# A hybrid diffusion network on one core: scans and projections dealt out block by block, and a new head ahead of them

## The chip, the cores and the metric

The kernel runs on one core of a Trainium2 chip. A core has a matrix engine (TensorE, PE in the profile), three engines for elementwise work (VectorE is DVE, ScalarE is ACT, GpSimd is POOL) and a queue that issues transfers (SyncE, SP); ScalarE and GpSimd can issue transfers too. The engines run side by side, each works through its own instructions in a fixed order, and they wait for each other by semaphores. TensorE writes to PSUM, eight banks of 512 numbers for each of 128 partitions; SBUF is the working memory. The metric is the time of one execution in microseconds (us).

## The reference, cut to what matters

Two layers work on 1024 latent tokens and 256 context tokens of width 1024. The first has a Mamba-2 mixer (SSD), the second attention, and a mixture of experts follows each. Only the first layer's mixer is touched here:

```python
h = rmsnorm(x, norm1_w) * (1 + scale) + shift     # shift, scale: silu(c) @ ada_w + ada_b
z, xbc, dtr = split(h @ in_w)                     # widths 2048, 4096, 64
xs, B, C = split(silu(dwconv(xbc, width=5)))      # 32 heads of 64; 8 groups of 128 states
dt = softplus(dtr + dt_bias); A = -exp(A_log)     # for a forward and a backward scan
y = scan_forward(xs, dt, A, B, C) + scan_backward(...) + D_skip * xs
out = rmsnorm(y * silu(z)) @ out_w
```

Each scan is chunked, with 128 tokens to a chunk. Inside a chunk y is a product of a decay matrix (times C·B) with x; between chunks a state is stepped on and read through C.

## The kernel before

All matrices are float32. A product of full precision is made of three: each operand is split into a rounded part and a remainder (`split`: ScalarE copies and rounds, VectorE or GpSimd subtracts), and `mm3` multiplies high by high, high by low and low by high.

**The head.** `ssd` loads the tokens in three blocks of 256, 512 and 512 (`BLK`), with transfers of 256 rows. `ada` makes shift and scale: eight pieces of the weights, 1 MB each, come through three buffers (`adw`), and each is multiplied as it lands. A loop over the ten token tiles makes the norm, scales on VectorE, transposes on TensorE and copies the result out of PSUM into `hf` (line 203 on ScalarE, line 205 on VectorE). Once shift and scale are known, a second loop modulates `hf` in SBUF (line 218, lines 216 for two of eight columns) and splits it into `hh` and `hl`, which every projection reads. Then follow `dt`: its projection (line 256), an eviction into `dT` by ScalarE, ten transposes (`dps`, line 261) to which VectorE adds `dtb` (`dt_bias`, line 262), and a long chain on VectorE that ends in the decays. The small loads for it, `dcol` (D), `dtb` and `nega` (A_log), stand on ScalarE's queue behind the modulation (lines 238, 245, 247).

**The projections.** `conv_tile` makes one tile of 128 channels: it loads and splits 512 KB of weights, and projects the three token blocks by `proj`, 24 matmuls each, into one of three PSUM banks (`in_ps`). ScalarE evicts each block twice (lines 358, 359). VectorE then runs the convolution: four passes over 1284 columns (line 363) and, around a tanh, two over 642 (line 368). `next(mods)` at its start advances the modulation for the rest of the layer by one piece.

**The scans.** There are eight groups. Each makes a B tile and a C tile, transposes B (`Btm`), multiplies C by B for each chunk (line 527, evicted into `cb`), and then for each of two pairs of heads makes an x tile and calls `core`. `core` transposes x (line 377), runs the backward states (lines 410, 396), and then goes through five pairs of chunks in seven iterations: `decays` for pair i (a transfer `Eb`, two selects on GpSimd, eight exponentials on ScalarE, an addition on GpSimd, a product with `cb` on VectorE, line 431: this gives M), `forward` for pair i (line 443 and the state's step, line 396), `entering` for pair i-1 (line 456: states read through C), and `output` for pair i-2: four y matmuls on M (line 474), an identity matmul that adds the entering part (line 477), and VectorE's `yd`, which is stored.

**The gates.** `gate` projects a tile of z, multiplies y with its silu, stores it and sums squares. Two of the sixteen (`early`) are made in the scans' pools after the last core, the rest behind them while `out_w` is loaded.

**What sets the order.** The program text is a trace of instructions. A scheduler then fixes each engine's queue ahead of time: it plays the trace against a cost model and gives an engine that is free the earliest traced instruction which the model holds to be ready and for which buffers are free. So matmuls traced later fill gaps that the model sees, but on the chip a queue waits for whatever stands at its front. `tc.issue_after(i)` places what is traced in its block behind instruction i on the same engine, in order only.

These lines of `core` are the ones that the change deals with:

```python
for i in range(len(pairs) + 2):
    if i < len(pairs):
        M[i] = decays(pairs[i])
        ent[i] = forward(pairs[i])
    ...
    if i >= 2:
        output(pairs[i - 2], M.pop(i - 2), yos.pop(i - 2), behind)
```

## Time and profile before

| | us |
|---|---|
| median of 3 runs (3855.78 to 3867.84) | 3864.43 |
| the profiled execution | 3858.05 |
| its span, first to last instruction | 3856.3 |

Busy in the span: TensorE 92%, VectorE 68%, ScalarE 53%, GpSimd 45%. The mean granted clock of TensorE was 0.973 of full speed.

In a row, L218 is line 218 of the kernel. PE is TensorE's matmuls, PEld its weight loads; a q behind an engine's name (SPq, ACTq) is its sequencer, which issues transfers. A matmul's end is modelled, so the rate of a stream is read from the starts. "A <- B" says that A's engine sat idle until B was done.

### The profile page before, as it was taken

The page shows a single profiled execution, that of the slowest core. Times are in us where ns is not written, and L with a number is a line of the kernel's source. Part 1 is how long each engine was busy: PE and PEld are TensorE (multiplying, and loading weights), DVE is VectorE, ACT ScalarE, POOL GpSimd, SP SyncE. Part 2 cuts the span into 40 slices and gives each one's busy share as a digit, 9 for nine tenths or more (in the row PEclk, how much of TensorE's full clock was granted, in tenths as well). Part 3 has the DMA queues.
Part 4 walks back from the last instruction along what each step waited for, and adds up shares of the span by engine and source line. Part 5 has one row for each costly group of instructions (what it writes and reads, how often), then busy time and mean ns, then how long its engine had stood idle before and what let it go on. Part 6 is the DMA issues. An engine that isn't in the chain of part 4 may idle for free.

```text
span 3856.3 us, 56522 instructions
## 1 busy us (share of the span) xinstructions
PE 3547.7 (92%) x21153; PEld 2674.9 (69%) x21153; DVE 2612.5 (68%) x3696; ACT 2026.0 (53%) x3325; POOL 1742.6 (45%) x1330
## 2 busy tenths in 40 slices
PE   5999999999899998999999999899999975999997
PEld 3767777777787775666666767677777654777765
DVE  4776777777634377666666665555666577999988
ACT  4545444544333223555555545477777534777665
POOL 1255444554443224566666652221111005777786
PEclk7999999999999998999999999999999987999999
DMA  4333322222544336888888873100000346999994
GB/s 174 105 109 125 118 92 78 83 85 84 154 139 152 110 128 234 307 317 317 320 321 302 289 236 94 36 15 1 1 1 12 132 168 235 378 381 376 352 339 165
DMA packets 296354, 681.07 MB, mean 177 GB/s; under 512 B 24192, under 2 KB 150000, under 8 KB 289936
## 3 DMA queue, kind: packets, MB, share of 16 engines
q1 hardware_dynamic: 269520, 615.50, 44.4%
q0 software_dynamic: 12720, 39.33, 4.2%
q10 hardware_dynamic: 13840, 22.63, 1.8%
q8 instruction: 167, 2.74, 0.3%
q14 instruction: 107, 0.88, 0.1%
HBM read 611.95 MB, written 62.82 MB: 175 GB/s over the span
## 4 chain that ended last, share of the span: by engine, by line
PE 38%; DVE 11%; issue 6%; POOL 4%; DMA 4%; ACT 2%; SPq 0%; ACTq 0%; POOLq 0%; DVEq 0%
DVE m_w L741 6%; PE pv L1189 5%; PE S L1155 4%; PE acc L54 4%; PE a_tr L1176 4%; PE acc L55 4%; PE acc L56 4%; PE cacc L710 4%; POOL m_w L739 3%; DMA m_raw<-in_moe_w_dram 3%; PE o_ps L55 1%; PE o_ps L56 1%; PE o_ps L54 1%; ACT m_w L736 1%; PE qkv L56 1%
## 5 line engine op out<-in xcount | busy, mean ns | idle before, releaser
L741 DVE TENSOR_TENSOR m_w<-m_raw,m_w 128x1792 fp32r<-128x1792 f32 (+1 forms) x384 | 889.7, 2340 | 242.3 <-ACT m_w L736 240.2
L736 ACT ACTIVATE m_w<-m_raw 128x2048 fp32r<-128x2048 f32 x384 | 732.7, 1916 | 477.8 <-DMA m_raw<-in_moe_w_dram 273.5
L739 POOL TENSOR_TENSOR m_w<-m_raw,m_w 128x256 fp32r<-128x256 f32 (+1 forms) x384 | 810.4, 2134 | 354.4 <-ACT m_w L736 353.1
L54 PE MATMUL in_ps<-hh,w 128*128 128x512 f32 (+1 forms) x1152 | 423.1, 367 | 10.9 <-DVE th L505 9.9
L55 PE MATMUL acc<-m_w,xl 128*128 128x512 f32 x1024 | 407.5, 398 | 22.9 <-DVE m_w L741 12.3
L56 PE MATMUL in_ps<-hh,w 128*128 128x512 f32 (+1 forms) x1152 | 420.2, 365 | 0.0
L55 PE MATMUL in_ps<-hl,w 128*128 128x512 f32 (+1 forms) x1152 | 418.3, 363 | 0.0
L54 PE MATMUL acc<-m_w,xl 128*128 128x512 f32 x1024 | 405.7, 402 | 3.0 <-ACT xl L48 2.0
L56 PE MATMUL acc<-m_w,xl 128*128 128x512 f32 x1024 | 402.4, 393 | 0.0
L427 ACT ACTIVATE Eb<-Eb,ebias 128x128 f32<-128x128 f32 x640 | 199.3, 391 | 166.4 <-POOL Eb L422 158.6
L1159 DVE TENSOR_REDUCE mx<-S 128x1 f32<-128x1024 f32 x128 | 155.7, 1217 | 182.1 <-PE S L1155 180.0
L54 PEld LDWEIGHTS in_ps<-hh,w 128*128 128x128 f32 x1152 | 220.0, 191 | 48.7 <-DVE th L505 10.9
L328 POOL TENSOR_TENSOR w<-w_raw,w 128x512 fp32r<-128x512 f32 x96 | 152.6, 1610 | 221.0 <-ACT w L325 210.7
L55 PEld LDWEIGHTS acc<-m_w,xl 128*128 128x128 f32 x1024 | 193.8, 189 | 82.9 <-DVE m_w L741 25.3
L1206 POOL TENSOR_TENSOR q<-s 64x128 f32<-64x128 f32 x128 | 58.5, 457 | 415.0 <-DVE mx L1164 340.2
L56 PEld LDWEIGHTS in_ps<-hh,w 128*128 128x128 f32 x1152 | 219.9, 191 | 31.0 <-issue 5.0
L55 PEld LDWEIGHTS in_ps<-hl,w 128*128 128x128 f32 x1152 | 219.8, 191 | 29.5 <-issue 4.3
L54 PEld LDWEIGHTS acc<-m_w,xl 128*128 128x128 f32 x1024 | 193.0, 189 | 67.3 <-issue 15.7
L56 PEld LDWEIGHTS acc<-m_w,xl 128*128 128x128 f32 x1024 | 193.9, 189 | 38.3 <-DVE xl L49 0.2
L55 PE MATMUL acc<-m_w,gT 128*128 128x512 f32 x512 | 203.8, 398 | 6.7 <-DVE m_w L741 4.1
L54 PE MATMUL acc<-m_w,gT 128*128 128x512 f32 x512 | 201.9, 400 | 1.3 <-ACT gT L48 1.3
L56 PE MATMUL acc<-m_w,gT 128*128 128x512 f32 x512 | 202.1, 395 | 0.1
(385 smaller groups left out, 7626.4 us busy)
## 6 DMA issues: line engine op xcount, KB each, us to landing
m_raw<-in_moe_w_dram SPq DMA_DIRECT2D x384, 1024.0 KB
adw<-in_ada_w_dram SPq DMA_DIRECT2D x48, 1024.0 KB
Eb<-fd SPq DMA_DIRECT2D x80, 512.0 KB
w_raw<-in_ssd_in_w_dram SPq DMA_DIRECT2D x48, 512.0 KB
ydd<-yd SPq DMA_DIRECT2D x80, 128.0 KB
yt_raw<-yzd SPq DMA_DIRECT2D x40, 256.0 KB
xs<-x SPq DMA_DIRECT2D x16, 512.0 KB
h<-h SPq DMA_DIRECT2D x16, 512.0 KB
```

The source lines that it names most:

```text
L54: mm(out, lhs[0], rhs[0], start=start, stop=False)
L55: mm(out, lhs[0], rhs[1], start=False, stop=False)
L56: mm(out, lhs[1], rhs[0], start=False, stop=stop)
L427: nc.scalar.activation(Eb[:, d, hh, cc], Eb[:, d, hh, cc], AF.Exp, bias=bias[:, c0 + cc, k:k + 1])
L710: nc.tensor.matmul(acc[32 * q:32 * q + 32], xc[:, k], raw[:, k % 2, 256 * q:256 * q + 256], start=(k == 0), stop=(k == KT - 1))
L736: nc.scalar.activation(w[0], raw, AF.Copy)
L739: nc.gpsimd.tensor_tensor(w[1][:, :, n:], raw[:, :, n:], w[0][:, :, n:].bitcast(F32), op=OP.subtract)
L741: nc.vector.tensor_tensor(w[1][:, :, :n], raw[:, :, :n], w[0][:, :, :n].bitcast(F32), op=OP.subtract)
L1155: nc.tensor.matmul(o, qTs[self.qt][:, 2 * self.hp + hh], kT[k][:, self.kv, 512 * b:512 * b + n], start=(k == 0), stop=(k == 1))
L1159: nc.vector.tensor_reduce(self.mx[:, 0:1], S[hh], axis=AX.X, op=OP.max)
L1176: nc.tensor.transpose(ps[:, q], self.pr[hh][:, (c0 + q) * P:(c0 + q + 1) * P], net.ident)
L1189: nc.tensor.matmul(self.pv[o:o + 64, 0], v32[:, t, self.kv], self.PT[:, t], start=(t < 2), stop=(t >= NT - 2))
```

## The change

1. The pool `cs` and the loads of `dt_bias`, `A_log` and D move ahead of the head. They land in parts of `wst`, which is not needed until the end of the `dt` chain. D is loaded as whole rows and set in place by two VectorE copies.
2. In the head all eight pieces of `ada` are traced first, then the tokens. The transposes of one column tile of a block share a PSUM bank (three banks instead of two), and the modulation reads that bank: ScalarE writes `hi`, VectorE the full value, and VectorE or GpSimd, in turns, the remainder.
3. `conv_tile` and `gate` become generators that yield after each token block. `core` takes such a sequence (`fill`), asks for one block at the start of each iteration but the first, and its y matmuls are placed behind that block's last matmul.
4. The tiles are reordered: B, C and x of group 0 come first; then the first core of a group carries the x tile of the second one and the next group's B; the second core carries the next group's first x tile and its C, in the last group the two early gates.

```diff
-            mod = self.ada(0, 0, npool, npool, ..., KT)
-            (tokens loaded between pieces of mod; copied out of PSUM into hf)
+        dtb, nega, dr = wst[:, 0], wst[:, 1], wst[:, 2, 0:HEADS]
+        nc.scalar.dma_start(dtb, rows(A["ssd_dt_bias"], [0, P], [1, 64]))
+        nc.scalar.dma_start(nega, rows(A["ssd_A_log"], [0, P], [1, 64]))
+        nc.scalar.dma_start(dr, rows(A["ssd_D"], [0, P], [1, HEADS]))
+            for _ in self.ada(0, 0, npool, npool, ..., KT):
                 pass
...
                 for j in range(KT):
-                    f, m = hf[b][:, j], int(b == 0)
+                    ps = pp.tile([P, 512], F32, name="x_tr")
+                    for i in range(n // P):
+                        nc.tensor.transpose(ps[:, i * P:(i + 1) * P], xx[:, i, j * P:(j + 1) * P], self.ident)
-                    if j in (2, 5):
-                        nc.scalar.activation(f, f, AF.Identity, scale=sc, bias=sh)
-                    else:
-                        nc.vector.tensor_scalar(f, f, sc, sh, op0=OP.mult, op1=OP.add)
-                    self.split(f, hh[:, j, t0:t0 + n], hl[b][:, j], nc.gpsimd if j in (1, 4) else nc.vector)
+                    nc.scalar.activation(hi, ps[:, :n], AF.Identity, scale=sc, bias=sh)
+                    nc.vector.tensor_scalar(f, ps[:, :n], sc, sh, op0=OP.mult, op1=OP.add)
+                    (nc.gpsimd if j % 2 else nc.vector).tensor_tensor(hl[b][:, j], f, hi.bitcast(F32), op=OP.subtract)
...
+                if b < 2:
+                    yield self.last
...
-                    for hh in range(2):
-                        nc.tensor.matmul(y[64 * hh:64 * hh + 64, cc], ...)
+                    with tc.issue_after(block.ins) if block else nullcontext():
+                        for hh in range(2):
+                            nc.tensor.matmul(y[64 * hh:64 * hh + 64, cc], ...)
...
             for i in range(len(pairs) + 2):
+                block = next(fill, None) if i else None
...
-                    output(pairs[i - 2], M.pop(i - 2), yos.pop(i - 2), behind)
+                    output(pairs[i - 2], M.pop(i - 2), yos.pop(i - 2), block, behind or block)
...
+        for _ in chain(tile_B(0), tile_C(0), tile_x(0)):
+            pass
         for g in range(NG):
-            conv_tile(16 + g, BT)
-            conv_tile(24 + g, CT)
...
-            for h in range(2):
-                conv_tile(2 * g + h, xT)
-                core(2 * g + h, xT, CT, Btm, cb)
+            more = g + 1 < NG
+            for h, fill in enumerate((chain(tile_x(2 * g + 1), tile_B(g + 1) if more else ()),
+                                      chain(tile_x(2 * g + 2), tile_C(g + 1)) if more else early_gates())):
+                core(2 * g + h, made.pop(2 * g + h), CT, Btm, cb, fill)
+                for _ in fill:
+                    pass
```

## Rows read from the trace of the kernel before

**Rows 1.** The page: each engine's busy time, its share of the span and its instructions.

```profile
PE 3547.7 (92%) x21153; PEld 2674.9 (69%) x21153; DVE 2612.5 (68%) x3696; ACT 2026.0 (53%) x3325; POOL 1742.6 (45%) x1330
```

**Rows 2.** The table by stretches, for the stage ahead of the scans and for the scans: stretch, its length, busy time of each engine with its instructions, granted clock, share of the DMA engines, GB/s.

```profile
0.00:112.00 112.00, 64.68 (x299) 40.17 (x300) 52.25 (x106) 46.16 (x90) 16.04 (x29) 0.77 0.46 164
112.00:1004.00 892.00, 828.15 (x5009) 650.25 (x5008) 649.33 (x1171) 428.96 (x1058) 427.35 (x489) 0.99 0.31 98
```

**Rows 3.** The same table for three stretches of the head.

```profile
0.00:44.00 44.00, 26.00 (x150) 12.98 (x150) 17.97 (x44) 22.42 (x45) 1.00 (x7) 0.88 0.92 344
44.00:70.00 26.00, 15.59 (x48) 11.51 (x48) 23.59 (x38) 14.98 (x30) 12.08 (x19) 0.67 0.12 34
70.00:92.05 22.05, 3.14 (x15) 2.78 (x15) 0.45 (x2) 2.90 (x5) 0.00 (x0) 0.59 0.13 35
```

**Rows 4.** The table of waits between 66 and 112 us: engine, tile and line, what it waited for, us in total, times, the longest.

```profile
DVE dtr L262 <- DMA ada_acc<-in_ada_b_dram: 23.8, 1, 23.8
...
PE dps L261 <- DVE dtr L263: 13.9, 1, 13.9
...
PE dps L261 <- ACT dT L258: 5.0, 1, 5.0
```

**Rows 5.** ScalarE's instructions in order of time: start, duration, what it is.

```profile
69.21 4.90 ACTq L245 DMA_DIRECT2D dtb<-in_ssd_dt_bias_dram  x1
```

**Rows 6.** The DMA queues between 60 and 100 us, ScalarE's queue: packets, MB, share of the engines.

```profile
q10 hardware_dynamic: 2384, 0.09, 3.2%
```

**Rows 7.** The table of TensorE's waits from 112 to 1050 us, columns as in rows 4.

```profile
PE y_ps L474 <- DVE Eb L431: 20.2, 26, 2.6
PE y_ps L474 <- issue: 17.0, 13, 1.7
PE tr_ps L527 <- DVE CT L368: 9.8, 7, 1.6
PE tr_ps L377 <- DVE xT L368: 8.1, 8, 1.2
...
PE st_ps L443 <- DVE H L396: 2.2, 6, 0.6
```

**Rows 8.** The table by stretches, cut at the first C·B matmul of a group: the longest group and the shortest of those without other work.

```profile
372.60:485.30 112.70, 104.88 (x635) 79.86 (x635) 79.79 (x145) 52.45 (x130) 53.29 (x63) 1.00 0.36 115
...
700.38:805.43 105.05, 97.39 (x603) 78.92 (x603) 77.01 (x141) 51.76 (x130) 52.96 (x63) 1.00 0.28 83
```

**Rows 9.** TensorE in order of time, in a group: projections of 256 columns behind transposes of B.

```profile
793.13 0.60 PE L377 MATMUL tr_ps<-ident,BT 128*128 128x128 f32 x4
...
794.04 0.28 PE L55 MATMUL in_ps<-hl,w 128*128 128x256 f32 x1
794.16 0.28 PE L56 MATMUL in_ps<-hh,w 128*128 128x256 f32 x1
```

**Rows 10.** TensorE in order of time: the last matmul of the `dt` projection (line 256), the first ones of B(0) (lines 54 to 56), the transpose behind the long wait, and B(0)'s last matmuls.

```profile
69.71 0.39 PE L256 MATMUL in_ps<-hl,w 128*128 128x512 f32 x1
...
75.56 0.41 PE L55 MATMUL in_ps<-hl,w 128*128 128x256 f32 x1
75.77 0.41 PE L56 MATMUL in_ps<-hh,w 128*128 128x256 f32 x1
...
92.05 0.44 PE L261 MATMUL dps<-ident,dT 128*128 128x128 f32 x1 [13.94 <-DVE dtr L263]
...
110.01 0.39 PE L55 MATMUL in_ps<-hl,w 128*128 128x512 f32 x1
110.24 0.39 PE L56 MATMUL in_ps<-hh,w 128*128 128x512 f32 x1
```

**Rows 11.** SyncE's queue in order of time: the first issue of tokens, and the last four pieces of modulation weights.

```profile
9.94 0.38 SPq L190 DMA_DIRECT2D xx<-in_ctx_dram  x1
...
15.10 21.64 SPq L119 DMA_DIRECT2D adw<-in_ada_w_dram  x4
```

**Rows 12.** The groups of instructions between 10 and 75 us (count, busy us, mean ns, idle time before them), and, first, the durations of line 218's products (shortest, median, longest in ns, first and last start in us).

```profile
L218 DVE TENSOR_SCALAR hf<-hf,scale,shift x18: 401/536/1585, 44.0 to 60.7; 128x512 f32<-128x512 f32 x12, 128x256 f32<-128x256 f32 x6
...
L49 DVE TENSOR_TENSOR hl<-hf,hh 128x512 fp32r<-128x512 f32 (+1 forms) x18 | 10.7, 650 | 0.0
L49 POOL TENSOR_TENSOR hl<-hf,hh 128x512 fp32r<-128x512 f32 (+1 forms) x6 | 8.5, 1430 | 6.6 <-ACT hh L48 6.6
L205 DVE COPY hf<-x_tr 128x512 f32<-128x512 f32 x10 | 6.9, 687 | 2.8 <-PE x_tr L200 2.8
L216 ACT ACTIVATE hf<-hf,shift,scale 128x512 f32<-128x512 f32 (+1 forms) x6 | 4.4, 728 | 0.0
```

**Rows 13.** The groups of instructions of the group from 700.38 to 805.43 us: ScalarE's exponentials, GpSimd's selects and addition, VectorE's convolution passes.

```profile
L427 ACT ACTIVATE Eb<-Eb,ebias 128x128 f32<-128x128 f32 x80 | 24.9, 392 | 21.6 <-POOL Eb L422 21.1 <-POOL xT L352 0.6
L422 POOL TENSOR_SCALAR_AFFINE_SELECT Eb<-Eb 128x512 f32<-128x512 f32 x20 | 18.9, 964 | 5.6 <-DMA Eb<-fd 5.6
L430 POOL TENSOR_TENSOR Eb<-Eb 128x512 f32<-128x512 f32 x11 | 17.0, 1547 | 1.6 <-ACT Eb L427 1.6
L363 DVE SCALAR_TENSOR_TENSOR xT<-raw,pcol,xT 128x1284 f32<-128x1284 f32 x8 | 14.2, 1778 | 4.9 <-ACT xT L359 4.8
L363 DVE SCALAR_TENSOR_TENSOR CT<-raw,pcol,CT 128x1284 f32<-128x1284 f32 x4 | 7.8, 1955 | 3.4 <-ACT CT L359 3.3
L368 DVE SCALAR_TENSOR_TENSOR xT<-raw,xT 128x642 f32<-128x642 f32 x4 | 3.2, 820 | 0.9 <-ACT raw L367 0.9
```

More of the change, by code (lines that the diff above doesn't have):

```diff
@@ L55, in mm3 @@
         mm(out, lhs[0], rhs[1], start=False, stop=False)
-        mm(out, lhs[1], rhs[0], start=False, stop=stop)
+        self.last = mm(out, lhs[1], rhs[0], start=False, stop=stop)
     def constants(self, es):
@@ new lines, in ssd @@
+        cs = tc.alloc_tile_pool(name="ssd_c", bufs=1)
+        bias, eF, wst, dec = (cs.tile([P, NT, 64], F32, name=n) for n in ("ebias", "eF", "wst", "dec"))
+        dcol = cs.tile([P, HEADS // 2], F32, name="dcol")
+        dtb, nega, dr = wst[:, 0], wst[:, 1], wst[:, 2, 0:HEADS]
+        nc.scalar.dma_start(dtb, rows(A["ssd_dt_bias"], [0, P], [1, 64]))
+        nc.scalar.dma_start(nega, rows(A["ssd_A_log"], [0, P], [1, 64]))
+        nc.scalar.dma_start(dr, rows(A["ssd_D"], [0, P], [1, HEADS]))
@@ L208, in ssd @@
+        for h in range(2):
+            nc.vector.tensor_copy(dcol[64 * h:64 * h + 64],
+                                  dr[64 * h:64 * h + 64].rearrange("p (j h) -> p h j", h=2)[:, h])
+        with tc.tile_pool(name="nrm", bufs=2) as npool, tc.tile_pool(name="nps", bufs=3, space=PSUM) as pp:
+            for _ in self.ada(0, 0, npool, npool, lambda: pp.tile([P, 512], F32, name="ada_ps", bufs=1), KT):
                 pass
@@ L225, in ssd @@
         adp = tc.alloc_tile_pool(name="ada", bufs=1)
-        cs = tc.alloc_tile_pool(name="ssd_c", bufs=1)
         gp = tc.alloc_tile_pool(name="grp", bufs=1)
@@ L229, in ssd @@
                                    for th in (1, 2))
-        bias = cs.tile([P, NT, 64], F32, name="ebias")
-        eF = cs.tile([P, NT, 64], F32, name="eF")
-        wst = cs.tile([P, NT, 64], F32, name="wst")
-        dec = cs.tile([P, NT, 64], F32, name="dec")
-        dcol = cs.tile([P, HEADS // 2], F32, name="dcol")
-        for h in range(2):
-            nc.scalar.dma_start(dcol[64 * h:64 * h + 64], rows(A["ssd_D"], [0, 64], [2, 16], off=h))
         with tc.tile_pool(name="dtp", bufs=1) as dp, tc.tile_pool(name="dtps", bufs=1, space=PSUM) as pp:
@@ L243, in ssd @@
             self.split(wdt[:, :, 0:64], wdh[:, :, 0], wdh[:, :, 1], nc.vector)
-            dtb = dp.tile([P, 64], F32, name="dtb")
-            nc.scalar.dma_start(dtb, rows(A["ssd_dt_bias"], [0, P], [1, 64]))
-            nega = dp.tile([P, 64], F32, name="nega")
-            nc.scalar.dma_start(nega, rows(A["ssd_A_log"], [0, P], [1, 64]))
             nc.scalar.activation(nega, nega, AF.Exp)
@@ L368, in conv_tile @@
                 nc.vector.scalar_tensor_tensor(dst[:, t0:t0 + n], th, 1.0, dst[:, t0:t0 + n], op0=OP.add, op1=OP.mult)
+            made[ci] = dst
+            yield self.last
         def transposed(src, name, pool):
@@ L397, in step, with core @@
                                                op0=OP.mult, op1=OP.add)
-        def core(ct, xT, CT, Btm, cb):
+        def core(ct, xT, CT, Btm, cb, fill):
             xtm = transposed(xT, "xtm", co)
@@ L467, in entering, with output @@
                 return yos, last
-            def output(c0, M, yos, behind):
+            def output(c0, M, yos, block, behind):
                 y = pst.tile([P, 2, P], F32, name="y_ps", bufs=2)
@@ L528, in ssd @@
                 nc.scalar.activation(cb[:, c0:c0 + n], ps[:, :n], AF.Copy)
[L529 to L547 removed]
+            more = g + 1 < NG
[3 more added lines that the diff above has]
+                for _ in fill:
+                    pass
+        acc0 = self.acc0
+        for p_ in (pst, ptp, pin, co, gp, adp, cs):
             p_.release()
@@ L562, in ssd @@
                 if ct >= early:
-                    gate(ct, weights(ct * P), zin, pair, self.acc, acc0 if ct == early else self.acc)
+                    for _ in gate(ct, weights(ct * P), zin, pair, self.acc, acc0 if ct == early else self.acc):
+                        pass
                 self.outw_part(ct, zp)
```

83 lines of the change are left out of this document (37 added, 46 removed).

## The prediction

> **What bounds the kernel now.** I began with the page: TensorE is busy for 92% of the span and no other engine for more than 68%, so a microsecond counts where TensorE waits or runs at the lower clock [rows 1]. The table by stretches then places the change. It touches the first 1214 us. The stage ahead of the scans (0 to 112 us) has TensorE busy for 64.7 of 112 us, the scans (112 to 1004 us) for 828.2 of 892 us [rows 2]. So there are 47 us to be had at the head and at most 64 us in the scans; the gates that follow keep their code, and from 1214 us on both kernels run the same code on the same data, which I take to be shifted and not changed.
>
> The head, cut finer, has three kinds of loss [rows 3]. Up to 44 us it loads: the DMA engines are busy for 92% of the time at 344 GB/s. From 44 to 70 us it modulates: VectorE is busy for 23.6 of 26 us and TensorE runs behind it. From 70 to 92 us nearly nothing runs: TensorE is busy for 3.1 of 22 us. The waits name the cause of that hole [rows 4]: TensorE waited 5.0 us for `dT` on ScalarE and 13.9 us for VectorE's `dtr`, which itself waited 23.8 us for a load (the view names an `ada_acc` load, but line 262 reads `dtb` and the sums). In order of time: ScalarE's queue stood for 4.9 us at the issue of `dtb` before it could evict `dT` [rows 5]; the load can have landed only shortly before TensorE went on at 92.05 us [rows 10], behind `dcol`, on a queue that moved 2384 packets and only 0.09 MB [rows 6]. Projection matmuls of B(0) stood ready behind the waiting transpose, so the hole is TensorE's own.
>
> In the scans the waits are small and many [rows 7]: 37.2 us before the y matmuls, because `Eb` (M) is not finished (20.2 us, and 17.0 us under "issue"); 9.8 us before C·B (line 527) for VectorE's CT; 8.1 us before the transposes of xT. A group of two head pairs takes 105 to 113 us with 97 to 105 us of TensorE work [rows 8]. The projections already lie between other matmuls, in runs [rows 9]; the change alters how they are dealt out, not whether they overlap.
>
> **The change part by part.**
> (1) *`dtb`, `nega` and D load at the start.* The three DMAs move ahead on ScalarE's queue into `wst`, where nothing has to come free first; D comes as rows of 32 numbers instead of 4-byte elements, for two small VectorE copies. From the last dt-projection matmul (69.71 us) to B(0)'s last matmul (110.24 us) there are 40.5 us [rows 10]. What lies in them: 24 matmuls of 256 columns at 0.12 us and 48 of 512 at 0.23 us (the spacing of starts at the full clock) make 13.9 us [rows 9, 10]; ten `dps` transposes and eight modulation matmuls some 2.2 us (an estimate, at 0.12 us each); and some 3 us because the first dozen matmuls run at the lower clock (0.21 us apart instead of 0.12). That is 19.1 us, so 21.4 us go. What is late next: C(0)'s weights, whose two buffers are free by then, and the dt chain on VectorE, which begins earlier by the same amount. Bounds: 15 us (if the 1 MB load for the next modulation, into space that the head gives free, makes TensorE wait once) and 24 us.
>
> (2) *Modulation.* Ahead of it, the load order changes, not the bytes, and the DMA engines are the bound: 15.1 MB in 44 us [rows 3]. Today x is issued at 9.9 us, after the constants' space comes free, and the last four pieces of weights wait behind it for 21.6 us [rows 11]. Now x needs no such wait. If it still slips in between the weights, modulation starts at about 42 to 44 us; if all eight weights go first, it starts near 30 us (8.4 MB at 344 GB/s, and some 3 us for the sum and its transposes), but then the squares and scalings of x, which today are hidden behind the loads, stand beside it. Modulating itself: VectorE gets 16 products of 512 columns out of PSUM at 0.69 us (the copy at line 205 is the nearest row) and 8 of 256 at some 0.40 us (an estimate: half of that and a fixed part), together 14.2 us, and 12 subtractions at 0.65 us, 7.8 us: 22.0 us against 23.6 us today [rows 3, 12]. GpSimd gets 12 subtractions instead of 6, at 1.43 us: 17.2 us beside it; ScalarE 24 at 0.73 us, 17.5 us. All 20 evictions go, but they were hidden behind the loads. So 1.6 us for certain and 0 to 10 us from the order; below nothing by 4 us if the transposes, now only three banks ahead, hold VectorE up. I take 5 us.
> A rule speaks against this part. VectorE's products of SBUF data, beside GpSimd's subtractions, took 0.54 us in the median, 0.40 us at the shortest and 1.59 us at the longest [rows 12]. The Trainium skill (SBUF — State Buffer, "Who interferes with whom") says that GpSimd and VectorE share one pair of ports which one instruction holds whole, among others against a VectorE operation with two SBUF inputs. By it the 7.8 us and the 17.2 us of subtractions could not overlap, the modulation would take 25 us, and part 2 would give 2 us instead of 5. No run here separates the two yet; I keep the sum by rows, and the 3 us lie inside its bounds.
>
> Head together: 26 us (11 to 34).
>
> (3) *Blocks of 24 matmuls between the scan's iterations, y bound behind them.* Nothing is added to the work: the same 34 projection tiles. A y pair now queues behind a block of 24 matmuls (2.9 us for 256 columns, 5.5 us for 512). No wait for M is longer than 2.6 us [rows 7], and M's chain for a pair (two selects of 0.96, eight exponentials of 0.39, an addition of 1.55 us, with a product at the end: some 7.5 us [rows 13]) has two iterations of at least 4 us each. So a wait that meets a block disappears: 15 of 16 cores have a block in all their output iterations, which makes 35 of the 37.2 us. What is queued behind the bound y: the identity matmul, then `yd` on VectorE, the store, and Eb's third buffer, needed three iterations later; I see no one who waits for that. But part of the lateness is GpSimd's and ScalarE's and stays: TensorE only reaches the next need of theirs earlier. I take 20 us of the 35 (bounds 0 and 35).
> (4) *xT is made a core ahead* (first three blocks of the core before): the 8.1 us of waits before line 377 go, seven of eight: 7 us (0 to 8).
> (5) *CT is finished last*, in the last iteration of the group before: its chain (four passes of 1.96 us and two shorter ones, about 10 us [rows 13]) ends as late before line 527 as now, with the next x tile's 13.9 us of blocks for cover. Without that cover it costs up to 10 us at each of seven boundaries; with it the 9.8 us stay. I take 0 (bounds: a gain of 10 and a loss of 30 us).
> (6) *Early gates as blocks of the last core*: today they are already used as filler there; 0.
>
> Scans: 27 us less (from 60 less, nearly all of the idle time, to 30 more). Sum: 3858.05 us (span 3856.3 and 1.75 us around it) less 26 less 27 is 3805 us. The median of the runs shown, 3864.43 us, is 6.4 us above this execution, so I predict 3811 us on that scale.
>
> **The rivals.**
> *Head alone.* The projections already lie in the scan's gaps [rows 9], and each engine's queue is fixed ahead by a cost model, so the misjudged moments may only move from y to line 527 or to the state steps. For it: the longest waits sit at ends of cores and of CT, where filler is on hand and still misplaced. Against: binding y is an order and not an estimate. Result: 3864 - 26 = 3838 us.
> *All idle time of the scans goes.* For it: VectorE has 77 of 105 us in a group, ScalarE and GpSimd half of it [rows 8]. Against: line 527 is not touched. Result: 3864 - 26 - 60 = 3778 us.
> *The convolution passes ahead on VectorE (slower).* The third block of a tile brings four passes of 1.78 and two of 0.82 us, 8.8 us on VectorE [rows 13], and they now stand in the program ahead of that iteration's state steps. A tile that ends in mid-core (15 of them) is followed by a block of 2.9 us and about 1.4 us of scan matmuls; then TensorE stands for 8.8 - 4.3 = 4.5 us until `H` is stepped. 15 times 4.5 is 68 us against the 53 us: 3864 + 15 = 3879 us. It decides from a hold of 3.5 us on. For it: VectorE is the second busiest engine. Against: today TensorE waits for line 396 for 2.2 us in all [rows 7].
> *The change doesn't do what it says:* if `dtb` still lands late, part 1 falls away and 3832 us remain. Nothing on ScalarE's queue speaks for it.
>
> **How the numbers follow.** Forecast 0.50 (its own range 3792 to 3830), head alone 0.20, everything 0.12, late `dtb` 0.03, VectorE rival 0.15. The range 3772 to 3858 leaves out about 0.05 below and 0.13 above. 0.3% is 11.6 us, about what a measurement can tell. Faster: the first four cases, 0.85, less 0.05 for a "head alone" at the low end of its bounds: 0.80. Those 0.05 and 0.04 of the VectorE rival, with a hold of 2.8 to 4.3 us, are "same": 0.09. The rest of that rival, 0.11, is slower.
>
> **What would show it.** Part 1: no wait of `dps` or `dT` above 1 us, B(0)'s last matmul at 80 to 88 us instead of 110. Part 2: VectorE's modulation 21 to 25 us long, ending before 67 us. Part 3: line 474's wait under 15 us; part 4: line 377's for xT under 2 us; part 5: line 527's at 7 to 15 us; a group at 99 to 104 us. The VectorE rival would show as waits of line 443 or 456 for line 396 above 30 us. It is wrong if 112 us of head shrink by less than 15 us, or if the groups get longer.

## The result, and the profile after

The changed kernel took 3880.07 us (median of 8 runs, 3873.95 to 3888.85) beside 3859.94 us for the kernel before: a ratio of 1.0054 (95% interval 1.0041 to 1.0067), 20 us slower where 53 us less were forecast. The profiled execution took 3888.72 us (span 3886.9), 8.7 us above its median; the one of before was 1.9 us below its own, so the two traces lie 30.6 us apart and not 20.

The table by stretches, as in [rows 2, 3]:

```profile
0.00:112.00 112.00, 82.66 (x363) 48.80 (x364) 60.69 (x110) 47.29 (x81) 27.45 (x36) 0.80 0.50 178
112.00:1004.00 892.00, 809.61 (x4822) 635.91 (x4822) 622.68 (x1119) 419.07 (x1031) 425.22 (x475) 0.97 0.30 93
...
70.00:92.00 22.00, 20.57 (x99) 13.61 (x99) 13.28 (x33) 9.30 (x14) 10.01 (x17) 0.93 0.29 97
```

The hole of 70 to 92 us is gone: TensorE is busy for 20.6 us of it instead of 3.1. In the next 892 us, though, it gets through 4822 matmuls instead of 5009. TensorE's waits from 80 to 1050 us, columns as in [rows 4], against [rows 7]:

```profile
PE tr_ps L546 <- DVE CT L356: 31.2, 7, 6.8
PE st_ps L400 <- DVE xw L374: 13.3, 15, 2.6
PE st_ps L433 <- DVE H L386: 11.1, 4, 4.5
PE y_ps L468 <- POOL yos L456: 10.9, 8, 1.8
PE y_ps L465 <- DVE Eb L421: 5.6, 6, 1.5
PE tr_ps L367 <- ACT xtm L368: 3.7, 1, 3.7
...
PE y_ps L465 <- issue: 2.2, 2, 1.2
```

Line 546 is C·B (527 before), 465 the y matmuls (474), 468 the identity matmul (477), 367 the transposes (377). The transposes' waits for xT are gone; the one of 3.7 us is for ScalarE's eviction of transposes ahead of it. The y waits fell from 37.2 to 7.8 us as forecast. But C·B now waits for CT for 31.2 us instead of 9.8, `xw`, `H` and `yos` have grown, and where no wait of the scans was longer than 2.6 us there are now waits of up to 6.8 us.

The groups show a second loss. Cut at the first C·B matmul of each group, the seven groups that can be cut so come to these sums, first of before, then of after, with a group of after that has long waits and one that hasn't:

```profile
sum 766.13, PE 712.33 PEld 557.35 DVE 548.73 ACT 376.51 POOL 383.36; mean PE 101.76 PEld 79.62 DVE 78.39 ACT 53.79 POOL 54.77
```

```profile
391.08:512.79 121.71, 107.16 (x635) 82.53 (x635) 82.03 (x145) 52.41 (x128) 58.21 (x62) 0.95 0.32 106
...
627.58:734.71 107.13, 97.68 (x603) 78.50 (x603) 76.59 (x141) 51.94 (x128) 53.81 (x63) 1.00 0.27 82
...
sum 808.44, PE 730.20 PEld 573.36 DVE 556.14 ACT 376.67 POOL 398.76; mean PE 104.31 PEld 81.91 DVE 79.45 ACT 53.81 POOL 56.97
```

42.3 us are lost: 24.4 us of idle time (78.2 instead of 53.8) and 17.9 us in which TensorE is busy for longer with nearly the same matmuls: the first of the seven groups has 665 after and 636 before, the other six together 3691 and 3695. These six alone lose 28.6 us, 17.1 of idle time and 11.5 of longer busy time. The granted clock says why TensorE is busy for longer: 0.95 in the long group, 1.00 in the other. Four rows of 3 us around the C·B at 512.79 us:

```profile
509.00:512.00 3.00, 0.00 (x0) 0.00 (x0) 0.71 (x1) 2.88 (x8) 1.22 (x1) 0.66 0.00 1
512.00:515.00 3.00, 2.21 (x9) 2.21 (x10) 1.47 (x2) 0.10 (x1) 0.21 (x4) 0.50 0.00 0
515.00:518.00 3.00, 3.00 (x15) 2.54 (x14) 1.29 (x2) 1.89 (x4) 0.00 (x0) 0.70 0.00 0
518.00:521.00 3.00, 3.00 (x19) 2.40 (x17) 0.69 (x1) 1.32 (x3) 0.10 (x1) 1.00 0.03 5
```

TensorE had stood since 506.0 us. The clock fell to its lower level (0.50, 1.2 GHz) at about 510 us, as the 0.66 of the first row says, and was back at full speed at about 516.8 us, by the 0.70 of the third: 4 us after TensorE had gone on. In the old order the idle time came in small pieces, with a clock of 0.99 over the scans [rows 2].

**The boundary of two groups**, in order of time (start, duration, what it is), engine by engine; the last three rows are a later boundary:

```profile
497.07 0.76 ACT L345 ACTIVATE CT<-in_ps,pcol 128x512 f32<-128x512 f32 x1
...
507.47 0.69 ACT L417 ACTIVATE Eb<-Eb,ebias 128x128 f32<-128x128 f32 x2 [6.52 <-POOL Eb L412]
...
510.53 1.36 ACT L355 ACTIVATE raw<-CT 128x642 f32<-128x642 f32 x2
...
497.87 9.07 DVE L351 SCALAR_TENSOR_TENSOR CT<-raw,pcol,CT 128x1284 f32<-128x1284 f32 x4
511.29 2.18 DVE L356 SCALAR_TENSOR_TENSOR CT<-raw,CT 128x642 f32<-128x642 f32 x2 [4.35 <-ACT raw L355]
...
498.27 2.30 POOL L420 TENSOR_TENSOR Eb<-Eb 128x512 f32<-128x512 f32 x1 [0.22 <-ACT Eb L417]
500.54 5.04 POOL L313 TENSOR_TENSOR w<-w_raw,w 128x512 fp32r<-128x512 f32 x2
505.54 2.49 POOL L412 TENSOR_SCALAR_AFFINE_SELECT Eb<-Eb 128x512 f32<-128x512 f32 x2
...
512.79 0.58 PE L546 MATMUL tr_ps<-CT,BT 128*128 128x128 f32 x1 [6.77 <-DVE CT L356]
...
727.74 3.74 POOL L412 TENSOR_SCALAR_AFFINE_SELECT Eb<-Eb 128x512 f32<-128x512 f32 x2
731.46 2.50 POOL L313 TENSOR_TENSOR w<-w_raw,w 128x512 fp32r<-128x512 f32 x2
...
734.71 0.49 PE L546 MATMUL tr_ps<-CT,BT 128*128 128x128 f32 x2 [2.77 <-DVE CT L356]
```

Read it backwards from 512.79. CT's last pass waits for its tanh (line 355). The tanh's input was ready at 506.9 us, but in ScalarE's queue eight exponentials (line 417) stand ahead of it; they wait for GpSimd's selects (line 412), and the selects stand behind 5 us of splitting the next B tile's weights (line 313). Besides, the four convolution passes took 2.27 us each where 1.54 us was the shortest; that alone delayed nothing here, since the tanh stood behind the exponentials for another 3.6 us. At the later boundary the selects stand ahead of the split, and C·B waits for 2.77 us. In the kernel before they stood ahead too:

```profile
476.92 2.63 POOL L422 TENSOR_SCALAR_AFFINE_SELECT Eb<-Eb 128x512 f32<-128x512 f32 x2 [2.27 <-PE tr_ps L377]
...
484.52 3.67 POOL L328 TENSOR_TENSOR w<-w_raw,w 128x512 fp32r<-128x512 f32 x2
...
485.30 1.16 PE L527 MATMUL tr_ps<-CT,BT 128*128 128x128 f32 x8 [1.33 <-DVE CT L368]
```

**The head.** SyncE's queue, to hold against [rows 11]:

```profile
1.65 22.25 SPq L119 DMA_DIRECT2D adw<-in_ada_w_dram  x8
23.95 0.43 SPq L201 DMA_DIRECT2D xx<-in_ctx_dram  x1
24.43 9.51 SPq L201 DMA_DIRECT2D xx<-in_x_dram  x4
```

All eight pieces of weights go first, so shift and scale are ready at 34.6 us; before, the modulation could begin only at 44.0 us [rows 12]. But the tokens are issued from 24 to 34 us, and their squares and scalings (10.4 us on ScalarE, 10.3 on VectorE) now lie for the most part inside the modulation (eight of the ten tiles), which lasts from 41.5 to 79.8 us. The `dt` projection ends at 79.81 us instead of 69.71 [rows 10], and what the early loads gave (from there to B(0)'s last matmul, 18.2 instead of 40.5 us) is half lost: 98.0 instead of 110.2 us.

### The profile page after: what moved, and what is told of

Same layout as the page of the kernel before. It is cut to its first block, busy times and chain, and to the rows that moved or that the text cites. A ratio compares the mean times of both kernels' runs of the same rounds, so it can differ in the third digit from the quotient of the medians.

```text
span 3886.9 us, 56482 instructions
## 1 busy us (share of the span) xinstructions
PE 3574.1 (92%) x21153; PEld 2687.2 (69%) x21153; DVE 2605.9 (67%) x3688; ACT 2024.5 (52%) x3310; POOL 1765.1 (45%) x1336
## 3 DMA queue, kind: packets, MB, share of 16 engines
q8 instruction: 167, 2.74, 0.3%
## 4 chain that ended last, share of the span: by engine, by line
PE 37%; DVE 11%; issue 6%; POOL 4%; DMA 4%; ACT 2%; SPq 0%; ACTq 0%; POOLq 0%; DVEq 0%
DVE m_w L750 6%; PE pv L1198 5%; PE S L1164 4%; PE a_tr L1185 4%; PE acc L54 4%; PE acc L56 4%; PE acc L55 4%; PE cacc L719 3%; POOL m_w L748 3%; DMA m_raw<-in_moe_w_dram 3%; PE o_ps L55 1%; PE o_ps L56 1%; PE o_ps L54 1%; PE qkv L56 1%; PE qkv L54 1%
## 5 line engine op out<-in xcount | busy, mean ns | idle before, releaser
L54 PE MATMUL in_ps<-hh,w 128*128 128x512 f32 (+1 forms) x1152 | 429.0, 372 | 11.8 <-DVE th L497 10.7
L56 PE MATMUL in_ps<-hh,w 128*128 128x512 f32 (+1 forms) x1152 | 428.9, 372 | 0.0
L54 PEld LDWEIGHTS acc<-m_w,xl 128*128 128x128 f32 x1024 | 192.9, 189 | 67.3 <-issue 15.7
```

What stands on the lines that cost most here:

```text
L54: mm(out, lhs[0], rhs[0], start=start, stop=False)
L56: self.last = mm(out, lhs[1], rhs[0], start=False, stop=stop)
```

## The experiments

Ratios are to the kernel before, run on the same chip.

**Which half costs.** Four kernels. `head_only` has the new head and the old scans, `scan_only` the reverse, `dt_early` only the early loads in the old kernel, `no_bind` the changed kernel with y not bound behind blocks:

```diff
# dt_early, in the kernel before (first lines)
+        dtb, nega, dr = wst[:, 0], wst[:, 1], wst[:, 2, 0:HEADS]
+        nc.scalar.dma_start(dtb, rows(A["ssd_dt_bias"], [0, P], [1, 64]))
...
-            dtb = dp.tile([P, 64], F32, name="dtb")
-            nc.scalar.dma_start(dtb, rows(A["ssd_dt_bias"], [0, P], [1, 64]))
# no_bind, in the changed kernel
-                    with tc.issue_after(block.ins) if block else nullcontext():
+                    with nullcontext():
...
-                    output(pairs[i - 2], M.pop(i - 2), yos.pop(i - 2), block, behind or block)
+                    output(pairs[i - 2], M.pop(i - 2), yos.pop(i - 2), block, behind)
```

> Only the new head (early loads of dt_bias, A_log and D; modulation out of PSUM, tokens loaded behind the modulation's weights), the scans as before. Theory 1 (the head gains, the scans' new order loses more): B(0)'s last matmul at about 98 us instead of 110, and 12 us less in all, ratio 0.997. Rival (what the head gains is given back before the first scan, since VectorE's dt chain ends no earlier): ratio 1.000. The prediction on record would have it at 0.993.

> Only the new order of the scans, the head as before. Theory 1: 33 us more than before, ratio 1.0085; TensorE's wait for CT at line 546's matmuls near 31 us instead of 10, its waits for xw and H near 27 us instead of 3, its wait for M near 8 us instead of 37. Rival (the loss comes from the head's shift, which moves the weights' transfers against the scans): ratio 1.000 to 1.003.

> Only the early loads of dt_bias, A_log and D; tokens, modulation and scans as before. If these loads alone were the hole of 70 to 92 us: B(0)'s last matmul at 87 to 92 us instead of 110, 20 us less in all, ratio 0.995, so better than the whole new head. If the hole was something else's too: 110 us, ratio 1.000.

> The changed kernel without the order of y behind a block; the blocks stay between the iterations. If the binding costs (it delays states' readers and yd): 10 to 20 us less than the changed kernel, ratio to before 1.000 to 1.003. If it is what removed the waits for M, and the loss is CT's place: the waits for M come back (20 to 37 us), ratio 1.008 to 1.012, the wait for CT stays near 31 us.

Measured: `head_only` 3839.13 us, 0.9965 (0.9953 to 0.9978); `scan_only` 3896.58 us, 1.0113 (1.0095 to 1.0130); `dt_early` 3839.11 us, 0.9964 (0.9948 to 0.9980); `no_bind` 3876.01 us, 1.0070 (1.0049 to 1.0091); the kernel before 3854.38 us. So by the medians the head gains 15 us (13 by the ratio), all of it by the early loads, and the scans lose 42 us, more than the 33 expected. The two don't add up exactly: 42 less 15 is 27 us, where the changed kernel lost 20; the intervals leave room for that. `no_bind` came out between its two theories, with an interval that overlaps the changed kernel's. Without the binding y waited no longer (the first row; the second, of the run with the new scans alone, shows CT's wait):

```profile
PE y_ps L465 <- DVE Eb L421: 5.3, 7, 1.2
```

```profile
PE tr_ps L561 <- DVE CT L371: 31.1, 7, 6.8
```

It is the new place of the blocks and tiles that took the y waits away, and the binding did nothing that can be measured. `dt_early` ended B(0) at 94.0 us, between its two theories; its head shows a price of the new load of D:

```profile
13.19 0.35 DVE L189 COPY dcol<-wst 64x16 f32<-64x16 f32 x2 [11.37 <-DMA wst<-in_ssd_D_dram]
...
13.19 8.95 SPq L200 DMA_DIRECT2D xx<-in_x_dram  x3
```

A copy on VectorE waits 11.4 us for D, with the constants' columns behind it, and the first tokens of x were issued 2.8 us later than in [rows 11], when D had landed. That is not all of the delay: SyncE's queue then stood for 7.7 us before a later issue of tokens, which the view puts down to the load of the `dt` weights (2.3 us before), and why that wait grew stays open.

**What makes the boundary late.** `c_first` swaps the two tiles of a group's second core, `w_dve` subtracts all weights' remainders on VectorE, `i0` deals a block out in a core's first iteration too:

```diff
# c_first
-  chain(tile_x(2 * g + 2), tile_C(g + 1)) if more
+  chain(tile_C(g + 1), tile_x(2 * g + 2)) if more
# w_dve
-                nc.gpsimd.tensor_tensor(w[1][:, sl], raw[:, sl], w[0][:, sl].bitcast(F32), op=OP.subtract)
+                nc.vector.tensor_tensor(w[1][:, sl], raw[:, sl], w[0][:, sl].bitcast(F32), op=OP.subtract)
# i0
-                block = next(fill, None) if i else None
+                block = next(fill, None)
```

> The changed kernel, but the second core of a group makes the next group's C tile first and the next x tile behind it (the change has x first, C last). Theory A, the end of a group is what is late (CT's convolution is finished on VectorE only when TensorE has already come to C by B, 31 us of waits at seven boundaries and most of the scans' 42 us): the wait of C by B for VectorE's CT falls from 31 us to under 10, groups get 3 to 5 us shorter, the time falls by 20 to 35 us against the changed kernel, to a ratio of 0.997 to 1.000 of the kernel before. Theory B, whichever tile is last is late (a tile's third block, its convolution and the exponentials of the last chunk pair stand on ScalarE and VectorE together): the CT wait goes but a wait of the xT transposes for the x tile of about the same size (20 to 35 us) takes its place, and the time stays within 8 us of the changed kernel, ratio 1.003 to 1.007.

> The changed kernel, but the remainder of the projection weights (line 313) is subtracted on VectorE instead of GpSimd. Theory C, GpSimd is what makes the boundary late: the convolution passes took 2.27 us each beside GpSimd's subtractions (2.5 us each) against 1.55 alone, and the selects stand behind the subtractions, so the exponentials and the tanh come late. By it the convolution passes return to about 1.6 us, the selects start some 5 us earlier, the wait of C by B for CT falls under 15 us and the time falls by 10 to 30 us (ratio 0.998 to 1.003). Theory D, VectorE's own queue is the limit: 60-odd subtractions of about 1.3 us are added to it, the wait for H or xw grows by 15 us or more, and the time stays or grows (ratio 1.005 to 1.012).

> The changed kernel, but a block of projections is also dealt out in a core's first iteration, so that the six blocks stand in iterations 0 to 5 and the last tile of a core ends one iteration earlier. Theory A (the last tile's convolution lacks one iteration of cover at the end of a core): the wait of C by B for CT falls from 31 us to under 12 us and the time falls by 15 to 30 us (ratio 0.998 to 1.002). Rival: the scan's own chains (M, H, xw) now lie bare in the last iteration, where no block covers them; the waits of y for M or of the yos matmul grow by 10 us or more and the time stays within 8 us of the changed kernel.

`c_first`: 3915.32 us, 1.0146 (1.0129 to 1.0163), above both theories' ranges. Theory B came nearer, though the next wait was not the one it named: C·B stands as long, now because ScalarE evicts the C·B ahead of it late, behind the same exponentials. `i0`: 3912.21 us, 1.0131 (1.0111 to 1.0150): CT's wait stayed (30.1 us), and `yos` and `xw` waits grew, as the rival said, at a higher price than it gave. `w_dve`: 3845.41 us, 0.9955 (0.9939 to 0.9971), 38 us below the changed kernel by the ratios, with C·B's wait for CT at 15.8 us: GpSimd is in it. Which of its subtractions?

```diff
# w_edge: the eight odd x tiles;  w_B: the seven B tiles of the scans and B(0)
-            w = weights(DI + ci * P)
+            w = weights(DI + ci * P, nc.vector if ci < 16 and ci % 2 else nc.gpsimd)
+            w = weights(DI + ci * P, nc.vector if 16 <= ci < 24 else nc.gpsimd)
```

> The changed kernel, with the remainder of the weights on VectorE for 8 of the 34 tiles alone, the x tile whose weights are split at the boundary of two groups (between the last blocks of CT and C by B). Theory E, the place is what counts (two GpSimd subtractions of 2.5 us stand there ahead of the selects, and slow the four convolution passes from 1.55 to 2.27 us): most of the 35 us that all 34 tiles gave is had with these eight, 20 to 35 us below the changed kernel, ratio 0.996 to 1.000. Rival, the load of GpSimd over the whole group counts: a quarter of it, some 8 us, ratio 1.002 to 1.005.

> As the run that moved eight of the 34 splits, but with the other eight: the remainder of the B tiles' weights, which the trace of that run shows between the last block of CT and C by B (5.05 us on GpSimd, the selects behind it), goes to VectorE. Place counts: the wait of C by B for CT falls from 31 us to under 18 us, the gaps of TensorE above 3.5 us (six in the scans of the change, 32.9 us) go to one or none, and the time falls by 20 to 35 us, ratio 0.996 to 1.000. Rival, GpSimd's load over the group: 8 us as with the other eight, CT's wait above 28 us, ratio 1.002 to 1.005.

`w_edge`: 3867.36 us, 1.0033 (1.0022 to 1.0045). I had taken the wrong tiles: in its trace 5.05 us of split still stand at the boundary, at 485.21 us, and they are the B tile's. That made it a control. `w_B`: 3852.11 us, 0.9979 (0.9970 to 0.9989). The waits of C·B, first of `w_edge`, then of `w_B`:

```profile
PE tr_ps L546 <- DVE CT L356: 35.3, 7, 6.7
```

```profile
PE tr_ps L546 <- DVE CT L356: 14.1, 7, 4.0
```

Eight splits moved either time, 8 us gained by the ones and 29 by the others: the place counts. Two causes were left at that place, the queue and the two engines slowing each other. `sel_first` moves an order on GpSimd and no work:

```diff
+                with tc.issue_after(behind.ins) if behind else nullcontext():
+                    nc.gpsimd.tensor_tensor(w[1][:, sl], raw[:, sl], w[0][:, sl].bitcast(F32), op=OP.subtract)
...
+            w = weights(DI + ci * P, sel.get(2) if 16 < ci < 24 else None)
...
+                    sel[c0 // 2] = nc.gpsimd.affine_select(Eb[:, d], Eb[:, d], pattern=[[0, 2], [0, 2], [sg, P]], base=0,
```

> The changed kernel; the only thing that moves is an order on GpSimd: the two halves of the B tile's split are bound behind the selects of the scan's third pair, which at the first four group boundaries stood behind them. GpSimd's work stays the same. Queue theory (ScalarE's exponentials of that pair stand ahead of CT's tanh in ScalarE's queue and wait for the selects, which wait for 5 us of split): at these boundaries the tanh starts some 5 us earlier, TensorE's gap before C by B falls from 4.5 to 6.8 us to under 3, and the time falls by 12 to 25 us (six long gaps, each with some 3 us of lost clock), ratio 0.999 to 1.0025. Contention theory (what delays CT is that the convolution passes take 2.27 instead of 1.55 us while GpSimd works): the passes still run beside GpSimd's selects and split, CT comes as late, ratio 1.004 to 1.007.

3858.46 us, 1.0002 (0.9989 to 1.0014): 20 us below the changed kernel, from a swap in GpSimd's queue. The wait of C·B over the seven boundaries, and the same boundary in its trace:

```profile
PE tr_ps L549 <- DVE CT L359: 15.2, 7, 2.8
```

```profile
484.33 0.76 ACT L348 ACTIVATE CT<-in_ps,pcol 128x512 f32<-128x512 f32 x1
...
491.02 1.86 ACT L420 ACTIVATE Eb<-Eb,ebias 128x128 f32<-128x128 f32 x6
492.96 1.37 ACT L358 ACTIVATE raw<-CT 128x642 f32<-128x642 f32 x2
...
485.12 7.76 DVE L354 SCALAR_TENSOR_TENSOR CT<-raw,pcol,CT 128x1284 f32<-128x1284 f32 x4 [0.57 <-ACT CT L348]
...
487.87 3.65 POOL L415 TENSOR_SCALAR_AFFINE_SELECT Eb<-Eb 128x512 f32<-128x512 f32 x2
491.50 4.32 POOL L314 TENSOR_TENSOR w<-w_raw,w 128x512 fp32r<-128x512 f32 x2
...
494.75 1.16 PE L549 MATMUL tr_ps<-CT,BT 128*128 128x128 f32 x8 [1.48 <-DVE CT L359]
```

From CT's last eviction to C·B it takes 10.4 us, in the changed kernel 15.7 us (497.07 to 512.79). Of these 5.3 us, 3.5 are the wait ahead of the tanh: it starts 0.1 us behind the passes (492.88) instead of 3.6 us (506.94 to 510.53). The passes themselves give 1.3 us (1.94 instead of 2.27 us each), and 0.5 us lie behind the tanh's start. The queue theory holds: contention alone was to leave the time where it was. Which of the two sets the tanh now, this run doesn't say, since the exponentials and the passes end together, at 492.88 us.

The three waits of 6.8 us came down to 1.5 us; the other four, 2.7 us each, where the selects had stood ahead of the split anyway, stayed. So the order on GpSimd makes about half of the scans' 42 us. The waits for `xw` (14.2 us), `H` (11.1) and `yos` (10.6) are as in the changed kernel, and what causes them was not taken apart.

**What undoes it.** `x_first` is the old scans with the new head, but loads the tokens between the weights and sets D in place later (not in the cut); `old_w` adds VectorE's subtraction to it, `best_new` has the same two edits on the new scans; `cover` also traces the first block of the group's second x tile ahead of C·B; `cover_pool` is `cover` with GpSimd's subtraction; `dummy` adds useless matmuls to the changed kernel.

```diff
# x_first
-            for _ in self.ada(0, 0, npool, npool, lambda: pp.tile([P, 512], F32, name="ada_ps", bufs=1), KT):
-                pass
+            mod = self.ada(0, 0, npool, npool, lambda: pp.tile([P, 512], F32, name="ada_ps", bufs=1), KT)
...
                     nc.sync.dma_start(xx[:, q:q + 2], src[q * P:(q + 2) * P].rearrange("(t p) d -> p t d", p=P))
+                    next(mod)
# cover
+            fills = [chain(tile_x(2 * g + 1), tile_B(g + 1) if more else ()),
+                     chain(tile_x(2 * g + 2), tile_C(g + 1)) if more else early_gates()]
+            next(fills[0])
             Btm = transposed(BT, "Btm", gp)
# dummy
+                with tc.issue_after(last.ins):
+                    ps = pin.tile([P, 512], F32, name="in_ps")
+                    for k in range(24):
+                        nc.tensor.matmul(ps, hT(0, 0, 1)[:, :P], hT(0, 0, 1), start=k == 0, stop=k == 23)
             Btm = transposed(BT, "Btm", gp)
```

> The scans of the kernel before; the head of the change, but x is loaded between the weights of shift and scale as in the kernel before (without waiting for the constants' space), the norms are made while those weights come, and D is put in place after the dt weights are split. Theory (the new modulation out of PSUM gains nothing because x was issued behind all eight weights, and the norms then stood beside the modulation): shift and scale at 38 to 41 us, modulation 20 to 25 us behind it, B(0)'s last matmul at 82 to 88 us instead of 95, time 7 to 13 us below that with the change's head (ratio 0.992 to 0.995). Rival (the modulation out of PSUM is itself no faster than the one in SBUF, 23.6 us, and the transposes three banks ahead hold it up): modulation of 28 us or more, B(0)'s last matmul at 92 to 97 us, ratio 0.996 to 0.998.

> The scans of the kernel before, the head with x between the weights, and the weights' remainder on VectorE. Theory E (the collision at the boundary belongs to the block order, and the old order has the splits lying where GpSimd has time): little to gain, -6 to +8 us against the same head with GpSimd's subtraction, ratio 0.992 to 0.997. Rival (GpSimd's subtraction costs the same in either order): 25 us or more below it, ratio under 0.988.

> The scans of the change, the head with x loaded between the weights, and the weights' remainder on VectorE throughout. If the two gains add (35 us from VectorE's subtraction, 4 to 5 us from the head), 3838 to 3842 us, ratio 0.993 to 0.995. If the block order of the scans were better than the old order once GpSimd is out of the way, it should come out below the old scans with the same two edits (next run but one); my theory is that it doesn't, since C by B still waited for CT for 15.8 us with the subtraction on VectorE.

> As the run with the scans of the change, the new load order and VectorE's subtraction, and besides the first block of the group's second x tile (24 matmuls of 256 columns, 2.9 us) is traced ahead of the transposes of B and of C by B, as cover for CT. If TensorE's place in the order is what is missing there, the wait of C by B for CT falls from about 16 us to under 4 and, since no gap of 3 us is left that lowers the clock, the time falls by 10 to 16 us against that run. If the block's own work (its evictions on ScalarE ahead of the tanh, its weights) pushes CT back by as much, the wait stays and the time is within 5 us of it.

> As the run with the x tile's first block ahead of C by B as cover, but with the weights' remainder on GpSimd again. If that cover alone is enough (2.9 us of the 4.5 to 6.8 us gaps, and the next weights split elsewhere), ratio 0.991 to 0.995. If the collision of GpSimd's subtractions with the selects and the convolution passes stays at the boundary, gaps of 3 to 4 us remain before C by B, ratio 0.997 to 1.002.

> The changed kernel with 24 matmuls of 512 columns added ahead of C by B in seven groups, whose result nobody reads (5.5 us each at the full clock), bound behind CT's last block. If the second half of the scans' loss is the clock that falls after each long gap (half speed for 4 to 8 us behind a gap of 4.5 to 6.8 us in this trace), added work that fills the gap makes the kernel faster: TensorE's gaps above 3.5 us go, the granted clock of the scans rises, and the time falls by 8 to 20 us (ratio 1.000 to 1.003). If the clock is no part of it, the time stays or grows by up to 10 us.

| | us | ratio (95%) |
|---|---|---|
| `x_first` | 3835.07 | 0.9942 (0.9924 to 0.9959) |
| `old_w` | 3832.87 | 0.9938 (0.9922 to 0.9955) |
| `best_new` | 3829.64 | 0.9942 (0.9925 to 0.9958) |
| `cover` | 3817.29 | 0.9910 (0.9893 to 0.9926) |
| `cover_pool` | 3877.61 | 1.0050 (1.0034 to 1.0067) |
| `dummy` | 3984.02 | 1.0327 (1.0310 to 1.0344) |

VectorE's subtraction is worth nothing in the old order (0.9942 and 0.9938) and was worth 38 us in the new one: the collision belongs to the block order. With it out of the way the two orders are equal (0.9938 and 0.9942). Only the cover then makes the block order better: CT's wait, 14.8 us in `best_new`, is all but gone, and `cover` is the fastest kernel here, 1.4% below the changed one:

```profile
PE tr_ps L557 <- DVE CT L363: 3.3, 4, 1.5
```

The cover without VectorE's subtraction gives nothing, against both theories: CT's wait falls to 3.4 us there too, but TensorE now waits for `Btm` (15.6 us, the longest 6.2) and for `H` (26.2 us at two lines). The named wait can be covered and the loss stays.

`dummy` was a miss: it added 40 us of matmuls (7 times 5.74) and 105 us of time, where at most 10 had been expected. The gap moved with them:

```profile
537.03 2.44 ACT L417 ACTIVATE Eb<-Eb,ebias 128x128 f32<-128x128 f32 x8 [9.04 <-POOL Eb L412]
539.38 0.57 ACT L368 ACTIVATE Btm<-tr_ps 128x512 f32<-128x512 f32 x1
...
540.01 1.12 PE L367 MATMUL tr_ps<-ident,BT 128*128 128x128 f32 x4 [6.22 <-ACT Btm L368]
```

The eviction of B's transposes, which the added matmuls had pushed back, came to stand behind the same exponentials. So it says nothing of the clock by itself, but shows that whatever is queued on ScalarE behind them is held. What the clock alone costs is argued from the sums above and wasn't isolated by a run.

In the head, `x_first` shows the modulation by itself: shift and scale at 45.75 us (38 to 41 expected), the first product on VectorE at 46.55, the last subtraction on GpSimd until 71.64, 25.1 us. Its groups of instructions from 30 to 80 us:

```profile
L219 DVE TENSOR_SCALAR hf<-x_tr,scale,shift 128x512 f32<-128x512 f32 (+1 forms) x24 | 16.7, 718 | 2.7 <-ACT hh L218 2.6
L220 DVE TENSOR_TENSOR hl<-hf,hh 128x512 fp32r<-128x512 f32 (+1 forms) x12 | 7.1, 594 | 0.0
...
L220 POOL TENSOR_TENSOR hl<-hf,hh 128x512 fp32r<-128x512 f32 (+1 forms) x12 | 16.6, 1385 | 7.8 <-DVE hf L219 7.8
```

B(0) ended at 89.9 us, between the theory (82 to 88) and its rival (92 to 97): beside `head_only` (95.2 us) the order of loads, together with the later copies of D, was worth 5 us. The modulation out of PSUM was worth no time that shows: from its first product to the last matmul of the `dt` projection `x_first` took 25.1 us, the kernel before 25.7.

## Why the prediction was wrong

**Part 1** was right as a mechanism and in size: 21.4 us were to go between the end of the `dt` projection and B(0)'s last matmul, 22.3 us went (40.5 to 18.2). One term was loose: "some 3 us" for a dozen matmuls at the lower clock, where 12 times 0.09 us is 1.1. What was missing is that the new loads reach back into the ones ahead: in `dt_early` the projection itself ended 6.4 us later (76.12 us), with the tokens of x issued later, the first of them by 2.8 us.

**Part 2** failed. I named the order that came, all eight weights first, and that the squares and scalings would then stand beside the modulation, but held the loss to 4 us. The `dt` projection ended 10.1 us later. The products took 0.70 us on average instead of 0.59 (16.9 us instead of 14.2): 0.81 us in the median of all, where I had taken 0.69 for 512 columns from the row of a copy. And the work on the tokens, which the loads had hidden, lay on ScalarE and VectorE between them. By rows I had 22.0 us for the modulation alone. By the Trainium skill (SBUF — State Buffer, "Who interferes with whom") GpSimd and VectorE take a shared port pair in turn, and I had worked out 25 us from it. `x_first` took 25.1 us, but that is luck on VectorE's side: its subtractions took 0.68 us for 512 columns beside GpSimd's, no more than with GpSimd idle (0.69 us), and it was the PSUM products that were longer. GpSimd's, which started some 0.16 us behind VectorE's each time, paid: 1.66 us, against 1.26 us at the shortest on as many columns (line 313 of the changed kernel).

The head together was to give 26 us. By the ratios it gave 13 (15 by the medians), and 22 (26) with the tokens loaded between the weights.

**Parts 3 and 4** came as forecast in the waits (y 7.8 us, forecast under 15; none left before the transposes of xT, forecast under 2) and failed in the sum. I wrote that part of the lateness "is GpSimd's and ScalarE's and stays", and took 20 of 35 us. All of it stayed, and more: C·B waited 21.4 us more, `H` 9 us more, and `xw` (13.3 us) and `yos` (10.9) came into the list. And the binding, which I held for the cause, was none.

**Part 5 is the step that decided.** I took 0 for it, with a loss of 30 us at most, although "without that cover" I had put up to 10 us on each of seven boundaries. VectorE's passes alone were in my chain of 10 us; I left out that the tanh is ScalarE's and stands in a fixed queue behind exponentials, and those behind GpSimd's selects. With the queue as it was, the chain took 15.7 us, three of the seven waits were 6.8 us, and with each the clock fell. The clock had no term in my sum of the scans at all, though [rows 3] show 0.59 where TensorE stood: the longer busy time that goes with it made 17.9 of the 42.3 us in the seven groups, and 11.5 of 28.6 in the six with as many matmuls as before.

**The slower rival** had the right sign and half the place: convolution passes ahead on VectorE. That its 3879 us lie 1 us from the measured 3880.07 is luck: the waits for `H` that were to show it (above 30 us) came to 11.1 us; TensorE stood before C·B. The rival that the misjudged moments "may only move from y to line 527 or to the state steps" had described it, and I had given it no loss.

## What to carry to other kernels

When the order of work is changed on the engine that sets the time, follow the next thing it needs back through every queue it passes, not only through the instructions that compute it: here a weight split on GpSimd held an activation on ScalarE that shares no data with it. Long waits cost more here than short ones of the same sum, since the clock fell with each of the six of 3.7 us and more and only with some of the shorter ones; count them with their longest, not by the total. A load put ahead of others isn't free: in `dt_early` other loads came later by it, and 6.4 of the 22.6 us that it had won before B(0)'s last matmul were lost again.

## What the runs showed of the hardware

Two things I had not expected. VectorE's convolution passes and GpSimd's work stretched each other: four passes took 9.07 us (1.54 us each at the shortest, 6.2 us), while the two splits took 2.52 us each (1.26 at the shortest). GpSimd's addition, which ran beside the first passes, took 2.30 us instead of 1.26. The Trainium skill's rule of part 2 (SBUF — State Buffer, "Who interferes with whom"), that the two engines take the shared ports in turn, comes near: in turn the passes, the splits and the addition make 9.9 us, and the passes were through in 9.07, with the splits done before that. Moved to VectorE, a split took 0.69 us in the median, half of GpSimd's.

And the clock fell with short gaps too, but not with all of them: of C·B's four waits of 2.7 us, the next 3 us were granted 0.54 behind the one at 734.71 us (2.77 us), and 1.00 behind the one at 842.52 us (2.72 us):

```profile
735.00:738.00 3.00, 3.00 (x13) 2.61 (x13) 2.44 (x3) 0.99 (x2) 0.94 (x4) 0.54 0.64 175
```

```profile
843.00:846.00 3.00, 3.00 (x22) 2.61 (x21) 2.57 (x3) 2.18 (x4) 0.76 (x4) 1.00 0.62 172
```

At 627.58 us (2.68 us) it stayed at 1.00 as well, at 948.81 us (2.74 us) it fell to 0.72 over the 3 us behind. In the kernel before it fell behind gaps of 1.6 us, 0.73 from 646 to 649 us. So among gaps of 1.6 to 2.8 us the length alone doesn't say, in these traces, whether the clock falls; with the six of 3.7 to 6.8 us in the scans of the changed kernel it fell every time.
